# Strassen's algorithm for 8 of 22 pairs of FFN gate/up groups in a two-layer hybrid trunk

## The chip, the cores and the metric

One core of one Trainium2 chip runs the whole computation. The metric is the device time of one execution in microseconds; lower is better. TensorE (PE) multiplies, VectorE (DVE) and ScalarE (ACT) do the element-wise work, GpSimd (POOL) and SyncE (SP) mostly issue DMAs.

## The reference

The input is 256 tokens of 2048 features in float32. Layer 0 has a gated DeltaNet mixer, layer 1 an HGRN2 mixer; each is followed by a SwiGLU FFN, with an RMSNorm ahead of each and residual adds. The change is in the FFN alone:

```python
def swiglu(h, w_gate, w_up, w_down):
    return (jax.nn.silu(h @ w_gate) * (h @ w_up)) @ w_down
...
for layer in range(DEPTH):          # DEPTH = 2
    h = h + mixer(rmsnorm(h, ...))
    h = h + swiglu(rmsnorm(h, ffn_norm[layer]), ffn_w_gate[layer], ffn_w_up[layer], ffn_w_down[layer])
return rmsnorm(h, final_norm)
```

The FFN is 5632 wide, so gate and up are 2048 x 5632 each, and down is 5632 x 2048.

## The kernel before

All weights stream once through the core in *halves*: 128 partitions x 1024 floats, 512 KB. `Trunk.stream` walks over a flat list of them. For each it loads `raw` (a ring of `RAW_BUFS` = 4 buffers, issued from SP), ScalarE copies it to `wh`, rounded to the format that TensorE multiplies, and VectorE makes the rest, `wl = raw - wh`; both have 4 buffers (`SPLIT_BUFS`). Each product of float32 matrices is three matmuls: high by high, high by low, low by high. The activations are split in the same way: `xt_h` and `xt_l` hold the normalized input, transposed.

A *group* of gate/up is 256 gate and 256 up columns (512 together): 8 halves, each with 2 tiles of 128 features x 2 token tiles x 3 = 12 matmuls of 512 columns (`mm_rows`), added up in the two banks of a `main` tile. There are 22 groups in an FFN. At the end of a group (`gate_up`, `end`) ScalarE computes `sg` = silu of the gate, scaled by 1/rms of the row (`rstd`), and VectorE multiplies it by the up part into `h1`. After two groups (a *pair*: 512 hidden features) VectorE transposes `h1` in 16 pieces (`turn`, 32 x 256 each) into `turned`, and the result is split into `hth` and `htl`. They are the operands of the down projection. That comes in two parts (`FF_PARTS`, 12 and 10 groups): after each part, four column groups `cg` of the output are computed, added to the residual `x` (loaded from and stored to `x_home` in DRAM, from Pool's queue), and at the end handed to the next layer.

All operations are first recorded, and `Recorder.plan` then puts them in order: for each engine it takes the operation that is ready by its estimates and is needed earliest, with the streaming matmuls in the order in which they were recorded. The order is fixed before the run; every engine works through its own queue and waits at its head.

Of the kernel before, what the change touches and what calls it, by code (L numbers as in the profile page):

```python
# [8 lines left out]
F32 = mybir.dt.float32  # L9
# [8 lines left out]
P = 128  # L18
# [6 lines left out]
FF_PARTS = (12, 10)  # L25
N_HGRN = 4
LEVELS = (64, 32, 16, 8, 4, 2, 1)
MASKED = LEVELS[2:]
AHEAD = 3
# [465 lines left out]
class Group:  # L495

    def __init__(self, chunks, mm, end, begin=None, apart=False, cols=False):
        self.chunks, self.mm, self.end, self.begin, self.apart = chunks, mm, end, begin, apart  # L500
        self.cols = cols
        self.halves = [
            c[:, at : at + 1024] for c in chunks for at in range(0, c.shape[1], 1024)
        ]


class Trunk:
# [22 lines left out]
    def apart(self):  # L530
        return self.aux(stream=True), self.aux(stream=True)

# [55 lines left out]
    def stream(self, groups):  # L588
        nc = self.nc
        flat = [(g, i) for g in groups for i in range(len(g.halves))]  # L590
        ready = {}

        def place(tag, g):
            w = self.tile(self.wsplit, [P, 1024], tag, F32R, ordered=True)
            v = nc.virtual(w)
            v.pad, v.cols = PAD, g.cols
            return w

        def load(n):
            g, i = flat[n]  # L600
            raw = self.tile(self.wraw, [P, 1024], "raw", ordered=True)
            nc.sync.dma_start(raw, g.halves[i])
            if n == 0:
                nc.ops[-1].lag = 4.2
                nc.edge(self.queue[1], nc.ops[-1])
            h = place("wh", g)
            nc.scalar.activation(h, raw, AF.Copy)
            low = place("wl", g)
# [4 lines left out]
        for n, (g, i) in enumerate(flat):  # L613
            while loaded < min(n + AHEAD, len(flat)):
                load(loaded)
                loaded += 1
            if i == 0:
                if g.begin:
                    g.begin()
                g.ps = self.apart() if g.apart else self.main()  # L620
            g.mm(g.ps, i, *ready.pop(n))
            if i == len(g.halves) - 1:
                g.end(g.ps)
# [143 lines left out]
    def turn(self, out, x):  # L767

        out = out.rearrange("p n (t a s) -> p t n a s", t=2, s=32)
        x = x.rearrange("p t (n b s) -> p t n b s", n=4, s=32)  # L770
        for a in range(4):
            for b in range(4):
                self.nc.vector.transpose(
                    out[32 * b : 32 * b + 32, :, :, a, :], x[32 * a : 32 * a + 32, :, :, b, :]
                )

    def ffn(self, j, after):
        nc, a = self.nc, self.a
        hts, h1s = {}, {}

        def gate_up(gi):
            def end(ps):
                if gi % 2 == 0:
                    h1s[gi // 2] = self.tile(self.pool, [P, 2, 512], "h1", bufs=2)
                h1 = h1s[gi // 2]
                for tt in range(2):
                    col = self.rstd[:, tt : tt + 1]
                    sg = self.tile(self.pool, [P, T], "sg", bufs=2)
                    nc.scalar.activation(sg, ps[:, tt, 0:T], AF.Silu, scale=col)
                    nc.vector.scalar_tensor_tensor(  # L790
                        out=h1[:, tt, gi % 2 * T : (gi % 2 + 1) * T], in0=ps[:, tt, T:512], scalar=col,
                        in1=sg, op0=ALU.mult, op1=ALU.mult,
                    )
                if gi % 2 == 0:
                    return
                turned = self.tile(self.pool, [P, 4, T], "turned", bufs=2)
                self.turn(turned, h1)
                hts[gi // 2] = ht, lt = tuple(
                    self.tile(self.pool, [P, 4, T], f"ht{x}", F32R, bufs=max(FF_PARTS) // 2) for x in "hl"
                )  # L800
                nc.scalar.activation(ht, turned, AF.Copy)
                nc.vector.tensor_tensor(out=lt, in0=turned, in1=ht.bitcast(F32), op=ALU.subtract)

            gu = a[f"ffn_gu{j}"]
            return Group(
                [gu[gi, i] for i in range(4)],
                lambda ps, i, h, l: self.mm_rows(ps, i, h, l, 4, self.operand), end,
            )

        def down(part, cg):  # L810
            first = sum(FF_PARTS[:part]) // 2
            n = FF_PARTS[part] // 2
            w = a[f"ffn_d{j}_{part}"]

            def operand(kt):
                h, l = hts[first + kt // 4]
# [12 lines left out]

            mm = self.mm_apart if apart else self.mm_rows  # L830
            return Group(
                [w[cg, i] for i in range(n)],
                lambda ps, i, h, l: mm(ps, i, h, l, n, operand), end,
                lambda: self.load_x(cg), apart,
            )

        groups = []
        for part, n in enumerate(FF_PARTS):
            lo = sum(FF_PARTS[:part])
            groups += [gate_up(gi) for gi in range(lo, lo + n)]  # L840
            groups += [down(part, cg) for cg in range(4)]
        groups[0].begin = lambda: self.enter(f"ffn{j}")
        return groups
# [439 lines left out]
    def gdn(self, after):  # L1283
        a = self.a
        states = [{} for _ in range(N_HG)]
        groups = []
# [4 lines left out]
        ba = Group([a["gdn_ba"]], self.mm_gates, gates_end)  # L1291
        cols = lambda chunks, end: Group(
# [3 lines left out]
        def part(hg):  # L1296
            st = states[hg]

            def kq_end(ps):
                self.gdn_qk(hg, self.conv_evac(ps), st)  # L1300
                self.gdn_inverse(hg, st)

            def v_end(ps):
                self.gdn_v(hg, ps, st)

            def z_end(ps):
                st["zs"] = zs = self.tile(self.pool, [P, 2, 512], "zs", bufs=2)
# [7 lines left out]
            rows = lambda name, end: Group(  # L1315
                w(name), lambda ps, i, h, l: self.mm_rows(ps, i, h, l, 4, self.operand), end
            )
            return [cols(w("gdn_kq"), kq_end), rows("gdn_v", v_end), rows("gdn_z", z_end)]
# [3 lines left out]
        for kind, n in GDN_ORDER.split():  # L1322
            n = int(n)
            groups += out[n] if kind == "o" else [parts[n]["kvz".index(kind)]]
        groups.insert(0, ba)
        groups[0].begin = self.gdn_setup
        return groups

    def out_proj(self, name, p, states, last, after):
# [9 lines left out]
        def make(cg):  # L1339
# [5 lines left out]
            return Group(  # L1345
# [5 lines left out]
        return [make(cg) for cg in range(4)]  # L1351
# [218 lines left out]
    def hgrn(self, after):  # L1570
        a = self.a
        states = [{} for _ in range(N_HGRN)]
        groups = []

        def part(g):
# [20 lines left out]
            cols = lambda kind, end: Group(  # L1596
                w(kind), lambda ps, i, h, l: self.mm_cols(ps, i, h, l, 2, 4, 4), end, cols=True
            )
            rows = lambda kind, end: Group(
                w(kind), lambda ps, i, h, l: self.mm_rows(ps, i, h, l, 4, self.operand), end  # L1600
            )
            return [cols(1, f_end), cols(0, q_end), rows(2, v_end), rows(3, z_end)]

        for g in range(N_HGRN):
            groups += part(g)
        groups[0].begin = self.hgrn_setup
        groups += self.out_proj("hgrn_out", 0, states, False, after)
        groups += self.out_proj("hgrn_out", 1, states, True, after)
        return groups
# [3 lines left out]
    def finish(self, cg):  # L1613
        nc = self.nc
        if cg == 0:
            self.last = self.tile(self.pool, [P, D], "last")
            nc.gpsimd.dma_start(self.last, self.a["final_norm"].broadcast_to([P, D]))
            self.y = self.tile(self.pool, [P, 2, D], "y")
# [15 lines left out]
    def finish_last(self, ps):  # L1634
# [4 lines left out]
        for tt in range(2):  # L1639
            t = lambda n, tag: self.tile(self.pool, [P, n], f"{tag}{tt}")  # L1640
            x, s3, ss, col = t(512, "xl"), t(1, "s3l"), t(1, "ssl"), t(1, "coll")
# [20 lines left out]
    def run(self):  # L1662
        self.setup()
        self.start(0, True)
        groups = self.gdn(self.next_input(1, False))
        groups += self.ffn(0, self.next_input(2, True))
        groups += self.hgrn(self.next_input(3, False))
        groups += self.ffn(1, self.finish)
        self.stream(groups)
# [92 lines left out]
```

## Time and profile before

| | |
|---|---|
| median of 3 runs | 2764.83 us (2764.65 to 2765.22) |
| profiled execution | 2763.82 us, its span 2761.4 us |
| PE, PEld, DVE, ACT, POOL busy | 99%, 84%, 69%, 52%, 9% |
| HBM read, written | 550.52 MB, 27.31 MB (209 GB/s over the span) |
| mean granted clock of TensorE | 0.999 |

The profile page lists busy times, a timeline in 40 slices, the chain of work that ended last, the costliest groups of instructions and the DMA issues. "wl<-raw,wh" reads: the instruction writes `wl` and reads `raw` and `wh`. Every operation is recorded by one helper, so that all have the same line (L490); they are told apart by the names of their tiles. "Landing" is the time from a DMA's issue to its completion.

### The profile page before, as it was taken

The page shows a single profiled execution, that of the slowest core. Times are in us where ns is not written, and L with a number is a line of the kernel's source. Part 1 is how long each engine was busy: PE and PEld are TensorE (multiplying, and loading weights), DVE is VectorE, ACT ScalarE, POOL GpSimd, SP SyncE. Part 2 cuts the span into 40 slices and gives each one's busy share as a digit, 9 for nine tenths or more (in the row PEclk, how much of TensorE's full clock was granted, in tenths as well). Part 3 has the DMA queues.
Part 4 walks back from the last instruction along what each step waited for, and adds up shares of the span by engine and source line. Part 5 has one row for each costly group of instructions (what it writes and reads, how often), then busy time and mean ns, then how long its engine had stood idle before and what let it go on. Part 6 is the DMA issues. An engine that isn't in the chain of part 4 may idle for free.

```text
span 2761.4 us, 41091 instructions
## 1 busy us (share of the span) xinstructions
PE 2744.9 (99%) x15662; PEld 2328.7 (84%) x15662; DVE 1899.6 (69%) x2857; ACT 1428.3 (52%) x2010; POOL 251.4 (9%) x370
## 2 busy tenths in 40 slices
PE   9999999999999999999999999999999999999998
PEld 9888888888888888888888989988888888888887
DVE  7787888887766667546665687778657675456764
ACT  6646666565554444344444556556454444344443
POOL 1213222232110000000000100000100000000000
PEclk9999999999999999999999999999999999999999
DMA  7686668787786666766667655555776666766664
GB/s 260 201 281 222 190 211 284 210 276 219 225 256 203 195 193 193 225 224 194 193 192 219 221 166 179 172 166 178 236 257 192 193 194 209 224 209 193 193 201 160
DMA packets 162677, 580.52 MB, mean 210 GB/s; under 512 B 20138, under 2 KB 21306, under 8 KB 162352
## 3 DMA queue, kind: packets, MB, share of 16 engines
q1 hardware_dynamic: 138912, 503.15, 57.1%
q0 software_dynamic: 23280, 73.91, 8.5%
q8 instruction: 122, 2.00, 0.3%
q10 hardware_dynamic: 288, 0.85, 0.1%
q14 instruction: 75, 0.61, 0.1%
HBM read 550.52 MB, written 27.31 MB: 209 GB/s over the span
## 4 chain that ended last, share of the span: by engine, by line
PE 98%; ACT 0%; DVE 0%; issue 0%; DMA 0%; SPq 0%; POOLq 0%; POOL 0%; ACTq 0%
PE main L490 92%; PE aux L490 6%; DMA first<-in_x 0%; ACT dec L490 0%; DVE wl L490 0%; ACT wh L490 0%; DVE utmp L490 0%; SPq L490 0%; DVE pre L490 0%; ACT xt_h L490 0%; DVE u L490 0%; ACT y L490 0%; POOLq L1758 0%; ACT junk L490 0%; DVE xl L490 0%
## 5 line engine op out<-in xcount | busy, mean ns | idle before, releaser
L490 DVE TENSOR_TENSOR wl<-raw,wh 128x1024 fp32r<-128x1024 f32 x945 | 1160.6, 1229 | 754.3 <-ACT wh L490 742.6
L490 ACT ACTIVATE wh<-raw 128x1024 fp32r<-128x1024 f32 x945 | 1000.9, 1060 | 1221.8 <-PE main L490 1123.5
L490 PE MATMUL main<-wh,xt_h 128*128 128x512 f32 x2176 | 849.3, 390 | 0.8 <-ACT wh L490 0.8
L490 PE MATMUL main<-wl,xt_h 128*128 128x512 f32 x2176 | 848.5, 390 | 1.3 <-DVE wl L490 1.3
L490 PE MATMUL main<-wh,xt_l 128*128 128x512 f32 x2176 | 849.5, 390 | 0.0
L490 PEld LDWEIGHTS main<-wl,xt_h 128*128 128x128 f32 x2176 | 408.5, 188 | 85.6 <-DVE wl L490 1.6
L490 PEld LDWEIGHTS main<-wh,xt_h 128*128 128x128 f32 x2176 | 408.5, 188 | 85.1 <-ACT wh L490 1.2
L490 PEld LDWEIGHTS main<-wh,xt_l 128*128 128x128 f32 x2176 | 408.6, 188 | 84.5
L490 PE MATMUL main<-xt_h,wh 128*128 128x256 f32 (+1 forms) x1040 | 288.8, 278 | 0.7 <-ACT wh L490 0.7
L490 PE MATMUL main<-xt_h,wl 128*128 128x256 f32 (+1 forms) x1040 | 288.3, 277 | 0.9 <-DVE wl L490 0.9
L490 PE MATMUL main<-xt_l,wh 128*128 128x256 f32 (+1 forms) x1040 | 288.1, 277 | 0.3 <-DVE xt_l L490 0.3
L490 PE MATMUL main<-wh,htl 128*128 128x512 f32 x664 | 258.6, 389 | 0.0
L490 PE MATMUL main<-wl,hth 128*128 128x512 f32 x664 | 258.4, 389 | 0.0
L490 PE MATMUL main<-wh,hth 128*128 128x512 f32 x664 | 258.3, 389 | 0.0
L490 PEld LDWEIGHTS main<-xt_h,wh 128*128 128x128 f32 (+1 forms) x1040 | 194.5, 187 | 1.3 <-ACT wh L490 0.9
L490 PEld LDWEIGHTS main<-xt_h,wl 128*128 128x128 f32 (+1 forms) x1040 | 194.4, 187 | 1.2 <-DVE wl L490 1.1
L490 PEld LDWEIGHTS main<-xt_l,wh 128*128 128x128 f32 (+1 forms) x1040 | 194.4, 187 | 1.0 <-DVE xt_l L490 0.5
L490 DVE STREAM_TRANSPOSE turned<-h 32x256 f32<-32x256 f32 x352 | 153.5, 436 | 7.2
L490 PE MATMUL main<-wh,ot_l 128*128 128x512 f32 x384 | 151.3, 394 | 0.0
L490 PE MATMUL main<-wl,ot_h 128*128 128x512 f32 x384 | 150.5, 392 | 0.0
L490 PE MATMUL main<-wh,ot_h 128*128 128x512 f32 x384 | 150.5, 392 | 0.0
L490 PEld LDWEIGHTS main<-wl,hth 128*128 128x128 f32 x664 | 124.6, 188 | 25.9
(206 smaller groups left out, 2249.9 us busy)
## 6 DMA issues: line engine op xcount, KB each, us to landing
raw<-in_ffn_gu SPq DMA_DIRECT2D x352, 512.0 KB, 4.7
raw<-in_ffn_d SPq DMA_DIRECT2D x176, 512.0 KB, 4.8
raw<-in_hgrn_in SPq DMA_DIRECT2D x128, 512.0 KB, 4.0
raw<-in_gdn_kq SPq DMA_DIRECT2D x64, 512.0 KB, 5.6
raw<-in_gdn_v SPq DMA_DIRECT2D x64, 512.0 KB, 4.7
raw<-in_gdn_z SPq DMA_DIRECT2D x64, 512.0 KB, 4.8
raw<-in_gdn_out SPq DMA_DIRECT2D x64, 512.0 KB, 5.0
x_home<-x POOLq DMA_DIRECT2D x36, 512.0 KB, 6.3
```

The lines of the kernel that those rows point to most:

```text
L490: getattr(getattr(tc.nc, op.eng), op.method)(*args, **kw)
```

## The change

Four of the eleven pairs of each FFN (1, 4, 7 and 8; with two FFNs 8 of 22) are computed by Strassen's algorithm, in the form with shared sums. The 2048 features are cut in two, the 256 tokens in two, and the pair's two groups are the two column blocks: 2 x 2 blocks on each side, seven block products where there were eight. The sums of input blocks (`mixh`, `mixl`) are made once at the start of an FFN, by VectorE and ScalarE, and need the row of 1/rms (`rstd_row`). The sums of weight blocks are made half by half as they stream: of the seven items for one place, three go in as loaded, two are added to by VectorE (`pre`), and two by a second DMA from Pool's queue that adds another half from DRAM to the loaded buffer (`accum_op`). These items have a ring of four buffers of their own (`sraw`); each feeds 6 matmuls. Their products go to four banks `aux` A to D; after the first 16 items three banks are copied aside (`between`), after all 28 the four blocks of the result are put together (`end`).

The items alternate with halves of other groups (`among`, `FF_PLAN`): pair 1 with pairs 2 and 3, pair 4 with the first part of the down projection, and so on. The down projection has three parts now (8, 8 and 6 groups). Eight of the eleven pairs are turned by 4 whole transposes on VectorE, a store to DRAM and four strip loads (`turn_through`); pairs 3, 6 and 10 (`FF_QUICK`) are turned on VectorE in two halves. The list of groups becomes a list of items, each with its own matmuls and ends.

```diff
-FF_PARTS = (12, 10)
+FF_PARTS = (8, 8, 6)
+FF_PLAN = (
+    "0 | 1:2,3",
+    "4:down | 7:5,6",
+    "8:down | 9 | 10",
+)
+FF_QUICK = (3, 6, 10)
...
+def among(few, many, tail):
+    out, done = [], 0
+    for i, item in enumerate(many):
+        out.append(item)
+        upto = min(len(few), -(-len(few) * (i + 1) // (len(many) - tail)))
+        out += few[done:upto]
+        done = upto
+    return out
...
         def load(n):
-            g, i = flat[n]
-            raw = self.tile(self.wraw, [P, 1024], "raw", ordered=True)
-            nc.sync.dma_start(raw, g.halves[i])
+            item = items[n]
+            raw = item.ring() if item.ring else self.tile(self.wraw, [P, 1024], "raw", ordered=True)
+            nc.sync.dma_start(raw, item.src)
...
+            if item.pre:
+                item.pre(raw)
...
+    def turn_through(self, out, x):
+        blocks = self.tile(self.pool, [P, 4, T], "blocks", bufs=1)
+        home = self.tile(self.dram, [P, 4, T], "blocks_home")
...
+        for b in range(4):
+            self.nc.vector.transpose(
+                blocks[:, b, :].rearrange("p (n t s) -> p n t s", n=4, s=32), x[:, :, :, b, :]
+            )
+        self.nc.gpsimd.dma_start(home, blocks)
+        home = home.rearrange("(a f) b r -> b f a r", a=4)
+        for b in range(4):
+            self.nc.gpsimd.dma_start(out[32 * b : 32 * b + 32], home[b])
+
+    def mix_inputs(self):
...
+        for q in range(2):
...
+            for cg in (q, 2 + q):
+                t = self.tile(self.pool, [P, 4, T], "turned", bufs=2, ordered=True)
+                tt(t, self.xt_h[cg].bitcast(F32), self.xt_l[cg].bitcast(F32), ALU.add)
+                tt(t, t, row, ALU.mult)
+                uv += [t[:, :, 0:P], t[:, :, P:T]]
+            a11, a21, a12, a22 = uv
...
+            tt(s1, a21, a22, ALU.subtract)
+            tt(s2, a11, s1, ALU.subtract)
+            tt(s3, a21, a11, ALU.subtract)
+            tt(s4, a12, s2, ALU.subtract)
...
+                nc.scalar.activation(h, sums[n], AF.Copy)
+                tt(low, sums[n], h.bitcast(F32), ALU.subtract)
...
+        def mixed_pair(pair):
...
+            def plus(of, other, kk):
+                def pre(raw):
+                    raws[of] = raw
+                    if other and other[0] == "+":
+                        nc.gpsimd.dma_start(raw, quarter(other[1:], kk), accum_op=ALU.add)
+                    elif other:
+                        nc.vector.tensor_tensor(out=raw, in0=raw, in1=raws[other], op=ALU.add)
+                return pre
...
+                ring = lambda: self.tile(self.pool, [P, 1024], "sraw", bufs=4, ordered=True)
+                return Item(src, mm, plus(of, other, kk), ring=ring)
...
+            def between():
...
+                nc.scalar.activation(sums["p1"], banks["A"], AF.Copy, scale=self.rstd[:, 0:1])
+                nc.vector.tensor_tensor(out=sums["u2"], in0=banks["B"], in1=sums["p1"], op=ALU.subtract)
+                nc.scalar.activation(sums["p5"], banks["C"], AF.Copy)
+                nc.scalar.activation(sums["p4"], banks["D"], AF.Copy, scale=self.rstd[:, 1:2])
...
+            for kk in range(4):
+                items += [
+                    item("11", None, kk, "A", plain(0, 0), True),
+                    item("12", "+11", kk, "C", mixed(1), True),
+                    item("22", "12", kk, "B", mixed(2), True),
+                    item("21", "22", kk, "D", plain(2, 1), True),
+                ]
+            items[0].begin, items[-1].end = begin, between
+            for kk in range(4):
+                items += [
+                    item("21", None, kk, "A", plain(2, 0), False),
+                    item("22", None, kk, "C", mixed(4), False),
+                    item("12", "+22", kk, "B", mixed(3), False),
+                ]
+            items[-1].end = end
...
-        groups = self.gdn(self.next_input(1, False))
-        groups += self.ffn(0, self.next_input(2, True))
+        items = self.gdn(self.next_input(1, True))
+        items += self.ffn(0, self.next_input(2, True))
```

How the queues stand now is shown at three places of the first FFN. The first is VectorE at the entry. Before, after the last `xt_l` (the transposed input's low part) of the gated DeltaNet's end:

```order
L490 TENSOR_REDUCE ss_62<-ssp_61 128x2
L490 TENSOR_SCALAR ss_62<-ss_62 128x2
L490 TENSOR_TENSOR wl_8949<-raw_8839,wh_8933 128x1024
L490 SCALAR_TENSOR_TENSOR xt_l_19_75<-aux_8930,head_63,xt_h_15_71 128x256 x2
L490 SCALAR_TENSOR_TENSOR xt_l_19_75<-aux_8938,head_63,xt_h_15_71 128x256 x2
L490 TENSOR_SCALAR rstdh_60<-rstd_59 128x2
```

Now, a little behind that place (`turned` holds an input block, `h_...` the sums of blocks, `sraw` a Strassen item's half):

```order
L496 TENSOR_TENSOR sraw_8900<-sraw_8900,sraw_8899 128x1024
L496 TENSOR_TENSOR wl_9035<-raw_8958,wh_9023 128x1024
L496 COPY rstd_row_65<-aux_9029 128x256
L496 TENSOR_TENSOR sraw_8901<-sraw_8901,sraw_8900 128x1024
L496 TENSOR_TENSOR turned_8889<-turned_8889,rstd_row_65 128x1024
L496 TENSOR_TENSOR wl_9062<-raw_8983,wh_9049 128x1024
L496 TENSOR_TENSOR turned_8890<-turned_8890,rstd_row_65 128x1024
L496 TENSOR_TENSOR wl_9080<-raw_9004,wh_9066 128x1024
L496 TENSOR_TENSOR h_1320_8891<-turned_8889,turned_8890 128x512
L496 TENSOR_TENSOR h_1321_8892<-turned_8889 128x512
L496 TENSOR_TENSOR wl_9101<-raw_9026,wh_9085 128x1024
```

Between two splits of plain halves there now stand one or two operations of the mixed inputs. The second place is VectorE in the middle of a stretch. Before, at the end of a pair's turn:

```order
L490 STREAM_TRANSPOSE turned_8888<-h_1337_8885 32x2x4x32 x2
L490 TENSOR_TENSOR wl_9368<-raw_9295,wh_9356 128x1024
L490 TENSOR_TENSOR htl_8890<-turned_8888,hth_8889 128x1024
L490 TENSOR_TENSOR wl_9387<-raw_9318,wh_9377 128x1024
L490 TENSOR_TENSOR wl_9408<-raw_9338,wh_9396 128x1024
```

Now, pair 1 beside pair 2, one round and the start of the next:

```order
L496 TENSOR_TENSOR wl_9420<-sraw_9295,wh_9404 128x1024
L496 TENSOR_TENSOR sraw_9364<-sraw_9364,sraw_9337 128x1024
L496 TENSOR_TENSOR wl_9440<-raw_9304,wh_9423 128x1024
L496 TENSOR_TENSOR wl_9448<-sraw_9337,wh_9434 128x1024
L496 TENSOR_TENSOR wl_9467<-raw_9352,wh_9454 128x1024
L496 TENSOR_TENSOR wl_9478<-sraw_9364,wh_9469 128x1024
L496 TENSOR_TENSOR wl_9500<-raw_9382,wh_9490 128x1024
L496 TENSOR_TENSOR wl_9510<-sraw_9394,wh_9502 128x1024
L496 TENSOR_TENSOR wl_9530<-raw_9414,wh_9520 128x1024
L496 TENSOR_TENSOR sraw_9462<-sraw_9462,sraw_9432 128x1024
L496 TENSOR_TENSOR wl_9549<-sraw_9432,wh_9535 128x1024
```

`sraw_9432` takes the buffer of `sraw_9295`, whose last reader is the first row here. Between that row and the addition that reads `sraw_9432` after its accumulating DMA stand eight operations. The third place is Pool's queue beside the first part of the down projection. Before, only the output's stores and loads:

```order
L490 DMA x_11361<-x_home_96 128x2x512
L490 DMA x_home_96<-x_11140 128x2x512
L490 DMA x_11582<-x_home_96 128x2x512
L490 DMA x_home_96<-x_11361 128x2x512
L490 DMA x_11803<-x_home_96 128x2x512
```

Now, with pair 4 in the same stretch:

```order
L496 DMA x_home_96<-x_8863 128x2x512
L496 DMA x_10666<-x_home_96 128x2x512
L496 DMA sraw_10637<-in_ffn_gu 128x1024
L496 DMA sraw_10804<-in_ffn_gu 128x1024
L496 DMA x_home_96<-x_9009 128x2x512
L496 DMA x_10906<-x_home_96 128x2x512
L496 DMA sraw_10900<-in_ffn_gu 128x1024
L496 DMA sraw_10993<-in_ffn_gu 128x1024
```

The accumulating DMAs (`sraw<-in_ffn_gu` on this queue) stand behind the pairs of store and load. Of the gated DeltaNet the order is the same as before up to its last output columns.

More of the change, by code (lines that the diff above doesn't have):

```diff
@@ L531, in apart, with group, first, opening @@
         return self.aux(stream=True), self.aux(stream=True)
+    def group(self, chunks, mm, end, begin=None, apart=False, cols=False):
+        ps, halves = [], halves_of(chunks)
+        def first():
+            if begin:
+                begin()
+            ps.append(self.apart() if apart else self.main())
+        items = [
+            Item(h, lambda wh, wl, i=i: mm(ps[0], i, wh, wl), cols=cols) for i, h in enumerate(halves)
+        ]
+        items[0].begin = first
+        items[-1].end = lambda: end(ps[0])
+        return items
+    def opening(self, items, setup):
+        first = items[0].begin
+        def begin():
+            setup()
+            first()
+        items[0].begin = begin
+        return items
     def setup(self):
@@ L612, in stream @@
         loaded = 0
-        for n, (g, i) in enumerate(flat):
-            while loaded < min(n + AHEAD, len(flat)):
+        for n, item in enumerate(items):
+            while loaded < min(n + AHEAD, len(items)):
                 load(loaded)
                 loaded += 1
[L617 to L623, printed above, removed]
+            if item.begin:
+                item.begin()
+            item.mm(*ready.pop(n))
+            if item.end:
+                item.end()
     def mm_rows(self, ps, i, wh, wl, n_chunks, operand, halves=range(2)):
@@ L794, in end @@
[L794 to L802, printed above, removed]
@@ L813, in down @@
+        def down(part, cg, pairs):
             w = a[f"ffn_d{j}_{part}"]
+            lo = sum(FF_PARTS[:part]) // 2
             def operand(kt):
-                h, l = hts[first + kt // 4]
+                h, l = hts[pairs[kt // 4]]
                 return h[:, kt % 4, :], l[:, kt % 4, :]
@@ L830, in down @@
             mm = self.mm_apart if apart else self.mm_rows
-            return Group(
-                [w[cg, i] for i in range(n)],
+            n = len(pairs)
+            return self.group(
+                [w[cg, p - lo] for p in pairs],
                 lambda ps, i, h, l: mm(ps, i, h, l, n, operand), end,
@@ L1349, in make @@
             )
-        return [make(cg) for cg in range(4)]
+        return [item for cg in range(4) for item in make(cg)]
     def hgrn_setup(self):
```

231 lines of the change are left out of this document (170 added, 61 removed).

## The prediction, on record before the changed kernel ran

> **What bounds the kernel now.** The page first: busy time, then the chain that ended last.
>
> ```profile
> PE 2744.9 (99%) x15662; PEld 2328.7 (84%) x15662; DVE 1899.6 (69%) x2857; ACT 1428.3 (52%) x2010; POOL 251.4 (9%) x370
> PE 98%; ACT 0%; DVE 0%; issue 0%; DMA 0%; SPq 0%; POOLq 0%; POOL 0%; ACTq 0%
> ```
>
> Only TensorE sets the end. Busy matmul time is modelled, so the second view is the chain in order of time: its longest pieces are the two FFNs, the place of the change.
>
> ```profile
> 828.78 636.50 PE main L490 x2808
> 2036.53 687.72 PE main L490 x3034
> ```
>
> That is 687.72/3034 = 0.2267 us per 512-column matmul, without a break (636.50/2808 gives the same). A weight half of a plain group has 12 matmuls: 2.72 us. The third view is the stretches: what the other engines have left.
>
> ```profile
> core 0: us, PE busy (x) PEld busy (x) DVE busy (x) ACT busy (x) POOL busy (x), PEclk, DMA share, GB/s
> 30.00:40.00 10.00, 10.00 (x90) 10.00 (x89) 6.53 (x13) 5.83 (x8) 1.02 (x3) 1.00 0.98 358
> 400.00:500.00 100.00, 100.00 (x687) 84.92 (x686) 84.83 (x184) 63.68 (x118) 33.50 (x51) 1.00 0.82 261
> 2100.00:2200.00 100.00, 100.00 (x443) 82.81 (x442) 65.33 (x81) 44.20 (x49) 0.00 (x0) 1.00 0.61 194
> ```
>
> In the FFN (2100 to 2200) VectorE is 65% busy, ScalarE 44%, and 194 GB/s come in. In the gated DeltaNet (400 to 500) VectorE runs at 85% while TensorE still has no gap, so 85% is bearable. The clock is full. The fourth view, the timeline of one weight half, shows how far ahead the splitting runs:
>
> ```profile
> 2153.09 1.06 ACT L490 ACTIVATE wh<-raw 128x1024 fp32r<-128x1024 f32 x1 [1.66 <-PE main L490]
> 2154.18 1.23 DVE L490 TENSOR_TENSOR wl<-raw,wh 128x1024 fp32r<-128x1024 f32 x1 [1.49 <-ACT wh L490]
> ```
>
> ScalarE waits for TensorE to free one of the four split buffers; 2155.41 - 2153.09 = 2.3 us later (2.5 with the hand-overs) the half is ready, and TensorE comes to it three halves later. Now the lead is 3 x 2.72 - 2.5 = 5.6 us.
>
> **The change, part by part.** *Matmuls removed.* A plain pair of groups has 16 halves x 12 = 192 matmuls; a Strassen pair has 28 items x 6 = 168. Eight pairs save 8 x 24 = 192; 192 x 0.2267 = **-43.5 us**, all on the bounding engine. Two FFN entries now also make the row of 1/rms: two small products each, by the nearest row 4 x 0.272 = **+1.1**.
>
> ```profile
> L490 DVE TENSOR_TENSOR wl<-raw,wh 128x1024 fp32r<-128x1024 f32 x945 | 1160.6, 1229 | 754.3 <-ACT wh L490 742.6
> L490 ACT ACTIVATE wh<-raw 128x1024 fp32r<-128x1024 f32 x945 | 1000.9, 1060 | 1221.8 <-PE main L490 1123.5
> L490 PE MATMUL aux<-head,x 128*128 128x128 f32 x112 | 14.5, 272 | 0.0
> L490 DVE STREAM_TRANSPOSE turned<-h 32x256 f32<-32x256 f32 x352 | 153.5, 436 | 7.2
> L490 DVE TENSOR_TENSOR x<-x,main 128x1024 f32<-128x1024 f32 x39 | 47.6, 1221 | 20.3 <-PE main L490 20.1
> L490 DVE TENSOR_TENSOR e<-b 128x512 f32<-128x512 f32 x48 | 31.4, 682 | 0.0
> ```
>
> *VectorE.* A Strassen item feeds only 6 x 0.2267 = 1.36 us of matmuls but costs one whole split (1.23 us), and two of four in its first half an addition of 1.22 us. Alone it would be bound by VectorE; that is why it stands between plain halves. Four items and four plain halves, as the order alternates them, are one round: 4 x 1.36 + 4 x 2.72 = **16.3 us** of TensorE, against 8 x 1.23 + 2 x 1.22 = 12.3 us of VectorE (75%). Over the kernel: 96 more splits +118 us, 64 additions +78, mixed inputs +41 (below), 5 sums of 0.68 for each of 8 pairs +27, 8 more output additions +10. Turns: now 352 x 0.436 = 153.5; then 16 pairs x 4 whole transposes = 28 and 6 x 32 half ones of at most 0.436 each, at least nothing: I take 0.3, 58 us; about -67. Sum about +207, so 2107 of 2730 (77%), under the 85% that is borne. On the path: nothing, as long as no wait stands in its queue. ScalarE gains 96 x 1.06 = 102 us and stays near 56%.
>
> *Entry of each FFN.* The mixed inputs are 8 operations of 1.22 and 16 of 0.68, 20.7 us. In the order's stretch from the first to the twentieth split, VectorE has 52 us of work (20 splits, these, two additions, the usual rest), TensorE 16 x 2.72 + 4 x 1.36 = 49.0. The 3 us that are missing are covered by the lead of 5.6; waits for 1/rms in the same queue take some of it. 0 to 6 us each, I take 2: **+4**.
>
> *Loads, and the loop through a buffer.* Each Strassen pair loads 28 halves for 16 (96 more on SP's queue), and 8 are added to by a DMA from Pool's queue. They have their own ring of four buffers, and in the first half the second item of each round passes the same buffer every round. The loop: load (L1), accumulating DMA (L2), then an addition and a split on VectorE (2.45) and hand-overs (about 0.45), and the buffer is free: c = L1 + L2 + 2.9. It holds TensorE up if c exceeds 16.3.
>
> ```profile
> raw<-in_ffn_gu SPq DMA_DIRECT2D x352, 512.0 KB, 4.7
> x_home<-x POOLq DMA_DIRECT2D x36, 512.0 KB, 6.3
> x<-x_home POOLq DMA_DIRECT2D x36, 512.0 KB, 5.7
> wide<-n_dram SPq DMA_DIRECT2D x32, 128.0 KB, 7.1
> ```
>
> Those are medians at moderate traffic. A round moves 8 loads + 1 accumulation + about 1.1 halves' worth of turns or x, some 10.1 x 0.524 MB = 5.3 MB in 16.3 us: 324 GB/s. The nearest stretches are two of about 16 us (436 to 452, then 606 to 622 us), each with its packets' line and its issues:
>
> ```profile
> DMA packets 1326, 4.78 MB, mean 299 GB/s; under 512 B 160, under 2 KB 160, under 8 KB 1325
> raw<-in_gdn_out SPq DMA_DIRECT2D x4, 512.0 KB, 6.0
> x_home<-x POOLq DMA_DIRECT2D x1, 512.0 KB, 6.4
> DMA packets 1300, 4.58 MB, mean 286 GB/s; under 512 B 187, under 2 KB 187, under 8 KB 1298
> raw<-in_gdn_z SPq DMA_DIRECT2D x4, 512.0 KB, 6.6
> before<-v_rows POOLq DMA_DIRECT2D x1, 512.0 KB, 9.6
> ```
>
> L1 is 4.7 to 6.6; I take 6.0. No accumulating DMA is in the trace. Below, L2 is a plain Pool load, 5.7; above, two plain transfers one behind the other, 5.7 + 6.3 = 12.0, since it must read the buffer too. I take the loaded plain one, 6.4, plus the time of half a MB at the stretch's own 358 to 299 GB/s less overlap, 1.2: 7.6, nearer to the low rows because most of a landing is latency. Then c = 6.0 + 7.6 + 2.9 = 16.5: 0.2 too long in each of the three returns between four rounds, and the lead (about 3.5 us with short items between) covers 0.6. **0 us** likely. In the second half (period 3 x 1.36 + 3 x 2.72 = 12.2) an accumulation comes into a buffer that a plain item left, so it binds later: two periods, 24.5, against c + 5 for the splits in between.
>
> *Pool's queue.* It stands in order. In the stretches beside the down projection the x load waits for the store before it:
>
> ```profile
> 1153.58 0.73 POOL L490 DMA_DIRECT2D x_home<-x  x1 [24.58 <-DVE x L490]
> 1160.46 0.72 POOL L490 DMA_DIRECT2D x<-x_home  x1 [6.15 <-DMA x_home<-x]
> ```
>
> Behind that wait of 6.15 us accumulations now stand queued, and TensorE behind them; the order leaves a round of work between, so I take nothing here and price it below. The turns through DRAM take a store and four strip loads, by the rows 6.3 + 7.1 + 4 issues, some 16 us, and are read more than 30 us later; where the reader is near (pairs 3, 6, 10) VectorE turns as before. Bank changes between the halves of a pair: 0 to 1 us a pair, I take 0.5: **+4**.
>
> *Sum.* Against the profiled execution's own 2763.82 (span 2761.4 and 2.4 around it): -43.5 + 1.1 + 4 + 0 + 4 = -34.4, so 2729.4. The median of the runs lies 1.0 higher (2764.83): **2730**.
>
> **Rivals.** *A: the accumulating DMA is slow and the loop paces TensorE.* For it: the transfer reads two sources, and no row prices it; the 9.6 us of one plain Pool load shows the tail. At the upper bound, c = 6.0 + 12.0 + 2.9 = 20.9; three returns of 4.6 less the lead of 3.5 = 10.3, and the second half (25.9 - 24.5)/2 x 4 = 2.8: 13.1 us for each of 8 pairs, 105 us, 2730 + 105 = **2835**, slower. It decides from 34.4/8 = 4.3 us a pair, that is c = 18.9, L2 about 10. Against it: all plain Pool medians lie at 5.7 to 6.4. The Trainium skill (Collectives: The Full Stack, section "The bandwidth ceiling: the fold count and why AG ≠ RS ≠ AR") says that an addition inside a DMA costs no cycles of its own, but two source reads through one ring, and so half the rate; no run here shows it. By that rule alone, doubling the whole 6.4 to an estimated 12.8, the sum would be slower still.
>
> *B: the DMA engines are full.* With the accumulation's second read a second-half period moves about (6 + 2 + 0.8) x 0.524 = 4.6 MB in 12.2 us, 378 GB/s; the fullest 10 us above carried 358 at a share of 0.98. At 358 that period takes 12.9: +0.66 x 4 x 8 = 21 us, **2751**, still faster. The Trainium skill (DMA: Bandwidth & Descriptors, "Where 436 GB/s comes from") puts HBM's limit for one core near the same 358, and the fabric's at 435.
>
> *C: Pool's order.* If each of four waits of 6.15 us in the four down stretches falls whole on a landed load, c is 22.6 once: 22.6 - 16.3 - 3.5 = 2.8 us, 16 times, 45 us: **2775**, slower.
>
> That the change doesn't do what it says can be left out: the order has 14212 matmuls for 14400.
>
> **Chances.** Forecast (2720 to 2742) 0.54; B 0.12; A 0.25, by where the plain rows lie; C, wholly or half, 0.07; gains and losses that cancel 0.02. About 0.2%, 5.5 us, is what a measurement can tell from no change. Faster is the forecast and B, 0.66; same is the last and half of C, 0.05; slower 0.29. The range goes from all costs at nothing (2722, rounded to 2720) up into A, to L2 near 11 (c = 19.9: 10.8 - 3.5 + 0.8 = 8.1 a pair, 65 us, 2795) and a little over: 2810. The rest of A, about 0.13, is left out.
>
> **What would show it.** Right: 192 matmuls fewer at 0.2267 each in the FFN stretches, TensorE without idle there, accumulating DMAs landing in 7 to 9 us, VectorE near 80%. Rival A: landings over 10 us, and TensorE idle behind VectorE and ScalarE, which wait for a DMA into sraw, mostly in the first half of a pair. B: a DMA share of 0.95 or more, with plain loads landing late too. C: such waits only beside the down projection. The forecast is wrong if TensorE's idle time in the two FFNs is over 40 us.

## The result, and the profile after

The changed kernel takes **2808.31 us** (median of 4 runs, 2806.01 to 2814.63); the kernel before took 2764.74 us (4 runs, 2763.53 to 2765.22) on the same chip. The ratio is 1.0162, 95% interval 1.0144 to 1.018: slower by 43.6 us, where 35 us less were forecast. The profiled execution took 2806.91 us, its span 2805.2.

Busy times on the page of the kernel after:

```profile
PE 2735.5 (98%) x15478; PEld 2298.7 (82%) x15478; DVE 2059.4 (73%) x3029; ACT 1537.7 (55%) x2152; POOL 366.3 (13%) x530
```

There are 184 matmuls fewer, which is the 192 and the added small products, but PE's busy time fell only by 9.4 us, and its idle time grew from 2761.4 - 2744.9 = 16.5 to 2805.2 - 2735.5 = 69.7 us. Where: the table by stage, the two FFNs up to the last gate/up half, first of the kernel before, then of the kernel after.

```profile
824.56:1546.28 721.72, 721.72 (x3201) 598.09 (x3200) 445.80 (x522) 318.22 (x351) 12.39 (x17) 1.00 0.65 205
2032.31:2751.06 718.75, 718.75 (x3176) 595.24 (x3175) 442.69 (x515) 312.57 (x339) 10.59 (x15) 1.00 0.63 200
```

```profile
824.05:1568.27 744.22, 716.93 (x3109) 583.50 (x3108) 525.66 (x608) 372.87 (x422) 69.31 (x97) 0.99 0.85 272
2054.31:2794.84 740.53, 714.81 (x3084) 580.68 (x3083) 522.98 (x601) 367.09 (x410) 67.44 (x95) 0.99 0.83 268
```

The first number is the stretch, the second PE's busy time in it. Before there was no gap; now TensorE idles 27.3 and 25.7 us, and the DMA share has gone from 0.65 to 0.85. The stages outside the FFNs kept their lengths. Landings, from the list of DMA issues of the kernel after (the last number is the median in us), and two groups of the table of waits (sum, count, longest):

```profile
raw<-in_ffn_gu SPq DMA_DIRECT2D x224, 512.0 KB, 5.9
sraw<-in_ffn_gu SPq DMA_DIRECT2D x224, 512.0 KB, 6.8
sraw<-in_ffn_gu POOLq DMA_DIRECT2D x64, 512.0 KB, 9.4
```

```profile
ACT wh L496 <- DMA sraw<-in_ffn_gu: 217.8, 47, 9.4
DVE sraw L496 <- DMA sraw<-in_ffn_gu: 61.3, 20, 8.0
```

The accumulating transfer lands after 9.4 us, and ScalarE, whose `wh` begins every split, waits for such blocks. One loop through a buffer can be followed in the timeline, pair 4 near its end; the load's buffer is known from the order's names. First SP's and Pool's issues, then the time that these two transfers took to land, from the list of DMA issues cut to them:

```profile
1093.47 0.33 SPq L496 DMA_DIRECT2D raw<-in_ffn_d  x1
1099.39 0.33 SPq L496 DMA_DIRECT2D sraw<-in_ffn_gu  x1
1100.53 0.33 SPq L496 DMA_DIRECT2D raw<-in_ffn_d  x1
1101.66 0.33 SPq L496 DMA_DIRECT2D sraw<-in_ffn_gu  x1
1102.80 0.33 SPq L496 DMA_DIRECT2D raw<-in_ffn_d  x1
1103.93 0.33 SPq L496 DMA_DIRECT2D sraw<-in_ffn_gu  x1
1106.20 0.33 SPq L496 DMA_DIRECT2D raw<-in_ffn_d  x1
...
1116.97 0.87 POOL L496 DMA_DIRECT2D sraw<-in_ffn_gu  x1 [10.88 <-ACT wh L496]
1128.62 0.33 SPq L496 DMA_DIRECT2D sraw<-in_ffn_gu  x1
```

```profile
sraw<-in_ffn_gu SPq DMA_DIRECT2D x1, 512.0 KB, 12.5
sraw<-in_ffn_gu POOLq DMA_DIRECT2D x1, 512.0 KB, 9.2
```

Then ScalarE and VectorE in the same 20 us:

```profile
1115.87 1.06 ACT L496 ACTIVATE wh<-raw 128x1024 fp32r<-128x1024 f32 x1 [1.66 <-PE main L496]
1126.28 1.06 ACT L496 ACTIVATE wh<-sraw 128x1024 fp32r<-128x1024 f32 x1 [9.36 <-DMA sraw<-in_ffn_gu]
1116.96 1.23 DVE L496 TENSOR_TENSOR wl<-raw,wh 128x1024 fp32r<-128x1024 f32 x1 [1.36 <-ACT wh L496]
1127.37 1.23 DVE L496 TENSOR_TENSOR wl<-sraw,wh 128x1024 fp32r<-128x1024 f32 x1 [9.19 <-ACT wh L496]
```

The load of 1103.93 lands at 1103.93 + 12.5 = 1116.4. The accumulation is issued at 1116.97, half a microsecond later (the view puts down as its releaser the `wh` that ended at 1116.93). It lands at 1126.2, `wh` starts at 1126.28, `wl` ends at 1128.60, and at 1128.62 the buffer is loaded again: 24.7 us where the prediction had c = 16.5. The item is the last of its pair, so it stands in the second half. For 9 us both splitting engines stand still with plain halves ready behind. What that costs TensorE, by the table of stretches there:

```profile
1117.00:1127.00 10.00, 6.99 (x31) 5.45 (x29) 1.19 (x1) 0.72 (x1) 2.44 (x3) 1.00 1.05 349
1127.00:1135.00 8.00, 6.85 (x22) 5.30 (x23) 7.63 (x8) 5.42 (x8) 0.00 (x0) 0.79 0.80 231
1129.00:1132.00 3.00, 3.00 (x8) 2.35 (x8) 3.00 (x4) 1.84 (x3) 0.00 (x0) 0.50 0.73 234
```

TensorE is idle for 3.0 us in the first stretch and 1.2 in the second. In the 8 us from 1127 on the granted clock is 0.79, and from 1129 to 1132 it is 0.50: a gap is paid once as idle time and again as slower matmuls.

### The profile page after: what moved, and what is told of

It is laid out like the page before. It is cut to its first block, busy times and chain, and to the rows that moved or that the text cites. A ratio compares the mean times of both kernels' runs of the same rounds, so it can differ in the third digit from the quotient of the medians.

```text
span 2805.2 us, 41692 instructions
## 1 busy us (share of the span) xinstructions
PE 2735.5 (98%) x15478; PEld 2298.7 (82%) x15478; DVE 2059.4 (73%) x3029; ACT 1537.7 (55%) x2152; POOL 366.3 (13%) x530
## 5 line engine op out<-in xcount | busy, mean ns | idle before, releaser
L496 ACT ACTIVATE wh<-raw 128x1024 fp32r<-128x1024 f32 x817 | 861.4, 1058 | 804.2 <-PE main L496 699.4
L496 DVE TENSOR_TENSOR wl<-raw,wh 128x1024 fp32r<-128x1024 f32 x817 | 999.9, 1226 | 400.9 <-ACT wh L496 392.7
L496 PE MATMUL main<-wl,xt_h 128*128 128x512 f32 x1664 | 653.2, 393 | 11.5 <-DVE wl L496 11.5
L496 PE MATMUL main<-wh,xt_h 128*128 128x512 f32 x1664 | 653.1, 393 | 4.9 <-ACT sg L496 4.1
L496 PE MATMUL main<-wh,xt_l 128*128 128x512 f32 x1664 | 652.7, 392 | 0.0
L496 ACT ACTIVATE wh<-sraw 128x1024 fp32r<-128x1024 f32 x224 | 236.7, 1058 | 303.0 <-DMA sraw<-in_ffn_gu 217.8
L496 DVE TENSOR_TENSOR wl<-sraw,wh 128x1024 fp32r<-128x1024 f32 x224 | 272.7, 1220 | 174.8 <-ACT wh L496 169.6
L496 PEld LDWEIGHTS main<-wh,xt_l 128*128 128x128 f32 x1664 | 314.2, 189 | 64.7
L496 PEld LDWEIGHTS main<-wh,hth 128*128 128x128 f32 x680 | 128.4, 189 | 32.1 <-ACT hth L496 5.4
L496 PEld LDWEIGHTS main<-wh,htl 128*128 128x128 f32 x680 | 128.1, 188 | 31.2 <-DVE htl L496 4.9
```

The lines of the kernel that those rows point to most:

```text
L496: getattr(getattr(tc.nc, op.eng), op.method)(*args, **kw)
```

## The experiments

Four theories. **1**: the loop through one of four buffers is too long for the round. **2**: the accumulating transfer burdens the DMA engines. **3**: accumulations wait in Pool's queue. **4**, formed after the first runs: the planner wrote the order for a landing of 6.5 us on Pool's queue (`LANDING`), so what needs a late block stands too early in ScalarE's and VectorE's queues and blocks what is behind it. The kernel before took 2763.1 to 2764.2 us beside each of these runs.

**What the second transfer costs.** e1: it overwrites and does not add. e2: it is left out. Both leave the weight sum out, 8 of 28 items of a pair.

```diff
-nc.gpsimd.dma_start(raw, quarter(other[1:], kk), accum_op=ALU.add)
+nc.gpsimd.dma_start(raw, quarter(other[1:], kk))          # e1; e2: no line
```

> The second transfer of the 8 items a pair overwrites instead of adding (the weight sums are left out there): same queue, same bytes from DRAM, same waits, only the addition's read of the buffer is gone. Theory 1 (the loop through a Strassen buffer: load 6.8 + accumulation 9.4 + 2.9 = 19.1 us against 16.3 of matmuls), with the second read as the slow part: landing falls from 9.4 to about 7.5, time to 2760-2780. Theory 2 (the DMA engines are full, every transfer is late): 8 half reads of about 76 a stretch less, landing stays at 8.5 or more, time 2790-2805. Theory 3 (Pool's order: accumulations stand behind turns and x loads): no change, 2800-2810.

> The second transfer is left out altogether (so the weight sums of those items are), all else stays. Theory 1: the loop is 6.8 + 2.9 = about 10 us, no wait is left, 2722 plus some 8 at the entries: 2725-2740. Theory 2: of the stretches' bytes some 12 to 20 percent go, plain loads still land late (6 to 7 us), 2750-2780. Theory 3: also 2725-2740, since nothing that matters stands behind the turns any more.

e1: 2748.49 us (ratio 0.9944, 0.9929 to 0.9959). e2: 2736.93 us (0.9902, 0.9887 to 0.9916). So everything else in the change comes near its forecast, and of the 71 us that the second transfers cost, 60 go with the addition in them. The overwriting transfer lands in 7.9 us, the accumulating one in 9.4.

**The additions on another engine.** e3 adds on VectorE, e6 on GpSimd, from a second block in SBUF that is loaded anyway.

```diff
-nc.gpsimd.dma_start(raw, quarter(other[1:], kk), accum_op=ALU.add)
+nc.vector.tensor_tensor(out=raw, in0=raw, in1=raws[other[1:]], op=ALU.add)   # e3
+nc.gpsimd.tensor_tensor(out=raw, in0=raw, in1=raws[other[1:]], op=ALU.add)   # e6
```

> All weight sums on VectorE: the accumulating DMA becomes an addition of the other buffer, which is still loaded (result complete). 64 more additions of 1.22 us, 78 us of VectorE, a round then has 8 x 1.23 + 3 x 1.22 = 13.5 of 16.3 us. Theories 1 and 3: loop gone, 2725-2745, under the time before. Theory 2: as without the second transfer, 2750-2780. A fourth, that VectorE is the next bound: VectorE over 88 percent busy in the stretches, 2750-2790, with TensorE waiting for wl and no DMA ahead of it.

> The 64 accumulating DMAs become additions on GpSimd of the buffer that is loaded already (result complete), 128x1024 each; no row shows such an addition, the plan's estimate is 2.4 us. Theories 1 and 3: the loop is 6 + 2.5 + 2.9 = 11.4 us, and VectorE gets nothing more: 2732-2750. If GpSimd's additions hold VectorE up while they run, VectorE's splits get longer than 1.23 us and the time is 2755-2790.

e3: 2762.70 us (median of 10 runs, 2757.12 to 2770.15; 1.000, 0.9988 to 1.0012): no gain is left. A stretch of e3 in the first FFN:

```profile
884.00:994.00 110.00, 108.11 (x478) 89.19 (x477) 89.24 (x93) 62.60 (x68) 5.53 (x10) 1.00 0.83 272
```

VectorE is 81% busy, its additions wait 102.7 us for blocks over the kernel, and TensorE has gaps (1.9 of 110 us). e6: **2750.05 us** (0.9949, 0.9934 to 0.9965), faster than before. An addition takes 2.83 us on GpSimd, and VectorE pays a little beside it (the blocks' splits of the kernel after first, 1220 ns, then the groups of e6):

```profile
L496 DVE TENSOR_TENSOR wl<-sraw,wh 128x1024 fp32r<-128x1024 f32 x224 | 272.7, 1220 | 174.8 <-ACT wh L496 169.6
```

```profile
L496 DVE TENSOR_TENSOR wl<-raw,wh 128x1024 fp32r<-128x1024 f32 x817 | 1048.7, 1286 | 425.1 <-ACT wh L496 415.8 <-PE aux L496 3.0 <-PE main L496 2.0
L496 DVE TENSOR_TENSOR wl<-sraw,wh 128x1024 fp32r<-128x1024 f32 x224 | 306.9, 1372 | 33.5 <-ACT wh L496 28.0
L496 POOL TENSOR_TENSOR sraw<-sraw,sraw 128x1024 f32<-128x1024 f32 x64 | 181.1, 2830 | 514.3 <-DMA sraw<-in_ffn_gu 453.1 <-DVE x L496 18.4 <-DVE h L496 16.4
```

**Half of the accumulations.** e7 does only the first half's additions on VectorE, e8 only the second half's; the others stay in DMAs.

```diff
+if other == "+22":     # e7; e8: "+11"
     nc.gpsimd.dma_start(raw, quarter(other[1:], kk), accum_op=ALU.add)
+else:
+    nc.vector.tensor_tensor(out=raw, in0=raw, in1=raws[other[1:]], op=ALU.add)
```

> Only the sums of the first half of a pair (12+11) go to VectorE; those of the second half stay accumulating DMAs. Theory 1 (a buffer that takes an accumulation each round, in the first half only): nearly all waits go, 2755-2770, with 32 additions more on VectorE. If every accumulating DMA costs alike: half of the way from 2808 to 2763, 2780-2790.

> The other way round: only the sums of the second half (12+22) go to VectorE; those of the first half stay accumulating DMAs. Theory 1: the loop of the first halves stays, 2790-2805. If every accumulating DMA costs alike: 2780-2790, as with the first halves.

e7: 2804.57 us (1.0145, 1.0129 to 1.0161); e8: 2819.09 us (1.0196, 1.0181 to 1.0212). With half as many accumulations the time is as long as with all, so the loss is not so much per transfer, and it is not in one half of the pair alone. But these runs do not price a transfer by itself: e3 shows that additions on VectorE cost time too, and the table under "What is left" shows how much in each half.

**A fifth buffer.** e4 makes its room by a block tile from the ring `turned`; e5 by keeping `u2` in a spare tile and one buffer less for `sg`.

```diff
-ring = lambda: self.tile(self.pool, [P, 1024], "sraw", bufs=4, ordered=True)
+ring = lambda: self.tile(self.pool, [P, 1024], "sraw", bufs=5, ordered=True)
```

> Five buffers in the ring of the Strassen items instead of four; to make room, the block tile of a turn comes from the ring of the turned tiles. All transfers stay. Theory 1: a buffer now comes round after five items, 20.4 us, over the 19.1 of the loop: most of the 86 us of waits go, 2735-2755. Theory 2: the engines are as full as before, 2790-2810. Theory 3: the waits behind turns stay, 2770-2790.

> Five Strassen buffers again, with the room taken elsewhere (one sum is kept in the dump tile of the square sums, the silu tile has one buffer), so that the turns are as in the changed kernel. All transfers stay. Theory 1 (the loop through one buffer, 19.1 us against 16.3): five items are 20.4 us, most of the first halves' waits go, 2745-2765. Theory 2 (the DMA engines are full): 2795-2810.

e4: 2810.55 us (1.0168, 1.0153 to 1.0183), but its turns came late (TensorE waited up to 11.6 us for `hth`), so its total tells little about the ring. e5: 2798.91 us (1.0129, 1.0113 to 1.0146), only 9 us better. ScalarE's waits for blocks went from 217.8 to 22.6 us, VectorE's additions now wait instead (91.8 us).

**The order, and both.** e9 tells the planner 9.0 us for an accumulating transfer; e10 does that with five buffers; e11 is e6 with five buffers.

```diff
 nc.gpsimd.dma_start(raw, quarter(other[1:], kk), accum_op=ALU.add)
+nc.ops[-1].lag = 9.0
```

> The whole edit: the planner that writes out the order is told 9.0 us instead of 6.5 us for the landing of an accumulating transfer; every addition stays with the transfers and the buffers stay four, so the order of VectorE, ScalarE and TensorE moves but no work does. Theory 4 (the order was written for 6.5 us, so splits and additions that need a late block stand at the head of VectorE's and ScalarE's queues and block the splits behind them): 2760 to 2780 us, and ScalarE's waits of wh for the DMA of sraw fall from 217.8 us to under 100. Theory 1 (a buffer's loop of 6.8 + 9.4 + 2.9 = 19.1 us against a round of 16.3 us): the loop is as long as before, 2795 to 2810 us, the waits move to SP's queue. Theory 2 (the accumulating transfers as such slow the loads): 2795 to 2810 us with raw still landing at 7 to 8 us in the stretches.

> The planner's 9.0 us for the accumulating transfer and a fifth buffer for block quarters together. If theory 4 and theory 1 each hold a part of the loss: 2740 to 2765 us, near the kernel whose second transfer only overwrites (2748.5 us). If theory 4 alone: as with the 9.0 us alone, within 5 us. If the accumulating transfers themselves hold the DMA engines (theory 2): 2785 us or more.

> The additions on GpSimd (2750.1 us with four buffers) and a fifth buffer. If late buffers are what is left over the kernel without second transfers (2736.9 us): 2738 to 2746 us. If what is left is the second load's traffic and the longer splits of VectorE beside GpSimd: 2746 to 2755 us, as with four.

e9: 2816.56 us (1.0184, 1.0167 to 1.0201), slower still. e10: **2749.48 us** (0.995, 0.9935 to 0.9964), with all additions in accumulating DMAs. e11: **2745.54 us** (0.9931, 0.9916 to 0.9945), the fastest complete version. Waits for blocks in e9, then in e10, and e10's landing:

```profile
ACT wh L496 <- DMA sraw<-in_ffn_gu: 151.3, 41, 7.6
DVE sraw L496 <- DMA sraw<-in_ffn_gu: 35.7, 17, 4.2
```

```profile
ACT wh L496 <- DMA sraw<-in_ffn_gu: 30.1, 19, 4.4
DVE sraw L496 <- DMA sraw<-in_ffn_gu: 25.9, 15, 4.4
...
sraw<-in_ffn_gu POOLq DMA_DIRECT2D x64, 512.0 KB, 8.6
```

The fitting order alone costs 8 us more, the fifth buffer alone brings 9, both together 59: on the total, theories 1 and 4 hold only jointly (by halves they part, see the table below). How long a loop is depends on the loads too, which bunch behind a stall. Loads matched to their accumulations: from a load's issue to its accumulation's in the kernel after, median 5.8 us in first halves and 9.2 (up to 14.6) in second halves. In the timeline above SP stands from 1093.8 to 1099.4, until a buffer is free, and then issues six loads in 7 us; the one at 1103.93 is the fifth of them, took 12.5 us, and made the next split late. A run that only spreads the loads was not made.

**What is left.** e12 is e10 with transfers that overwrite (the 8 of 28 sums left out); e13 and e14 are e7 and e8 with the 9.0 us.

> As the kernel with 9.0 us for the accumulating transfer and five buffers (2749.5 us), but the second transfer overwrites the buffer and does not add (8 of 28 weight sums of a Strassen pair are left out). If only the latency of an accumulating transfer costs anything, and five buffers with the order that fits have hidden it (theories 1 and 4): within 5 us of 2749.5 us. If the addition in the transfer also takes time from the DMA engines (theory 2): faster by 8 us or more, under 2742 us.

> First-half additions on VectorE, second-half ones by accumulating transfers that the planner takes as 9.0 us, four buffers. With the order for 6.5 us this took 2804.6 us. By the prediction's loop arithmetic the second half binds only from a loop of 19.5 us, and here it is 5.9 + 9.2 + 2.9 = 18.0, so if the order was what cost (theory 4) it falls to 2750 to 2770 us. If four buffers are too few in the second half as well: 2795 us or more.

> The other way round: second-half additions on VectorE, first-half ones by accumulating transfers that the planner takes as 9.0 us, four buffers. With the order for 6.5 us this took 2819.1 us. If the loop through a buffer in the first half (18.2 us or more, against a round of 16.3 us) is what paces TensorE (theory 1), the fitting order does not help: 2790 us or more. If the order alone decided (theory 4): 2750 to 2775 us.

e12: 2733.49 us (0.9892, 0.9877 to 0.9906). With five buffers and 9.0 us an overwriting second transfer costs nothing that shows (e2, without any, took 2736.93); one that adds takes 2749.48 - 2733.49 = 16 us more. That is what theory 2 foretold, but the traces do not put it on full DMA engines: e10 still waits 30.1 + 25.9 us for blocks (above), e12 4.2 us, and the table below finds the difference in the first halves alone. The same 120 us of the first FFN in e10, then in e12:

```profile
884.00:1004.00 120.00, 119.64 (x528) 98.76 (x528) 94.05 (x107) 67.71 (x74) 14.60 (x22) 1.00 0.96 307
```

```profile
884.00:1004.00 120.00, 120.00 (x531) 99.41 (x530) 95.12 (x110) 68.47 (x74) 12.62 (x23) 1.00 0.91 304
```

The issues and landings of the second transfers, in e10 and then in e12 (of an issue group the second number is the mean in ns that it holds Pool's queue):

```profile
L496 POOL DMA_DIRECT2D sraw<-in_ffn_gu x64 | 56.8, 888 | 643.5 <-DMA sraw<-in_ffn_gu 341.6 <-DVE wl L496 128.3 <-DVE sraw L496 74.9
```

```profile
PE 2706.5 (99%) x15478; PEld 2293.5 (84%) x15478; DVE 2075.3 (76%) x3029; ACT 1550.2 (57%) x2152; POOL 343.1 (13%) x530
L496 POOL DMA_DIRECT2D sraw<-in_ffn_gu x64 | 35.2, 550 | 645.6 <-DMA sraw<-in_ffn_gu 315.0 <-DVE wl L496 202.8 <-DVE sraw L496 51.5
sraw<-in_ffn_gu POOLq DMA_DIRECT2D x64, 512.0 KB, 7.6
```

At about the same GB/s the accumulating version holds the DMA engines at a share of 0.96 for 0.91. e13: 2785.52 us (1.0076, 1.0047 to 1.0105); e14: 2780.99 us (1.0066, 1.0051 to 1.0081). Both missed: the fitting order brings 19 and 38 us, less than theory 4 alone would give and more than theory 1 alone.

How the loss splits can be read from the starts of the Strassen matmuls (those that write `aux`) in each profiled execution. A first half runs from the first matmul of item 1 to that of item 17, a second half from there to the last matmul of item 28. The table has the time beyond that of e12, in us, summed over the eight pairs; the rest of the span is in the last column.

| | buffers, planner's landing | second transfers | first halves | second halves | rest |
|---|---|---|---|---|---|
| after | 4, 6.5 | all add | 22.4 | 42.5 | 6.7 |
| e9 | 4, 9.0 | all add | 31.0 | 53.7 | -0.8 |
| e5 | 5, 6.5 | all add | 38.5 | 0.0 | 23.0 |
| e10 | 5, 9.0 | all add | 12.0 | 0.1 | 1.6 |
| e1 | 4, 6.5 | all overwrite | 14.9 | 0.8 | -2.2 |
| e7 | 4, 6.5 | second half; first on VectorE | 16.1 | 47.2 | 5.2 |
| e13 | 4, 9.0 | second half; first on VectorE | 17.1 | 33.2 | 4.3 |
| e8 | 4, 6.5 | first half; second on VectorE | 46.4 | 35.1 | 2.5 |
| e14 | 4, 9.0 | first half; second on VectorE | 34.8 | 11.8 | -3.4 |

In the second halves the ring decides: with a fifth buffer nothing is lost, whatever the order (e5, e10, and e4 as well), with four the fitting order does not help while all the transfers add (e9), and with four and the shorter landing of an overwriting transfer (7.9 us, e1) almost nothing is lost. In the first halves it takes both: the buffer alone (e5) and the order alone (e9, e14) leave over 30 us, both leave 12. The second half of pair 1 in the kernel after, in e5 and in e10:

```profile
935.36:987.29 51.93, 47.99 (x205) 38.58 (x204) 29.20 (x32) 25.77 (x29) 6.34 (x10) 0.98 0.96 298
942.18:988.20 46.02, 46.02 (x205) 38.10 (x204) 29.44 (x30) 26.99 (x29) 6.33 (x9) 1.00 1.00 323
934.34:980.35 46.01, 46.01 (x204) 38.11 (x203) 31.20 (x34) 26.82 (x29) 6.32 (x9) 1.00 1.02 326
```

With five buffers the DMA engines are at a share of 1.00 and more there, and TensorE has no gap. Whether a sixth buffer would take what is left of the first halves in e10 stays open.

## Why the prediction was wrong

- *Matmuls removed* (-43.5): right. e12, with the same matmuls, is 30.0 us faster than before, against -34.4 forecast with entries and bank changes (+4 each). By the matmul starts of e12 the two entries cost 3.0 us, the bank changes show no gap over 0.5 us, and the down projections that begin beside pairs 4 and 8 wait 2.2 us each for `hth` and `htl`: four times, 8.9 us that the sum did not have.
- *VectorE* (2107 us, 77%): right in kind, 2059.4 us. The half transposes came out at 303 ns (192 of them, 58.1 us), as taken. That 85% is borne did not carry over: at 81%, with waits for blocks in VectorE's queue, e3 lost the gain; which of the two it was, no run parts. In the kernel after VectorE is 71% busy in the FFNs, and waits for `wh`.
- *Loads, and the loop through a buffer* (0 us): **this is the step that failed.** It took c = 6.0 + 7.6 + 2.9 = 16.5 us in both halves, and the loads as even. L2 measured 9.4. L1, from a load to its accumulation's issue, measured 5.8 in first halves but 9.2 in second ones, where loads bunch. So in the second half c = 9.2 + 9.4 + 2.9 = 21.5, over the 19.5 from which the prediction's own formula binds: (26.5 - 24.5)/2 x 4 = 4.0 us a pair, 32 for eight, and 42.5 were measured (with the slower clock behind the gaps). The formula holds there: in e1, measured in the same way, c = 7.3 + 7.9 + 2.9 = 18.1 stays under 19.5, and 0.8 us were lost. In the first half c = 5.8 + 9.4 + 2.9 = 18.1 gives 3 x 1.8 - 3.5 = 1.9 us a pair, 15 for eight, and 22.4 were measured. But there the formula does not tell it all, since five buffers alone did not help (e5): the order, written for a landing of 6.5 us, holds up splits behind late blocks (VectorE's additions wait 91.8 us for them in e5 and 25.9 in e10), and for that the sum had no term.
- *The clock* had no term either. In span, the kernel after is 2805.2 - 2733.6 = 71.6 us longer than e12: 69.7 - 27.1 = 42.6 more of idle TensorE and 2735.5 - 2706.5 = 29.0 more of busy time for the same 15478 matmuls. Of these 29.0, about 14 are the clock, by the mean granted clock of each (0.993 of 2805.2 us and 0.998 of 2733.6). The rest is stalls that the page counts as busy, since it draws a matmul of 512 columns with 0.39 us where the next starts 0.23 us behind it.
- *Rival A* named this mechanism, and the stated range reaches up to 2810 only because of it; that 2808.3 lies inside is no success of the forecast. Rival A's signs came in part. TensorE's idle time did stand behind waits for a DMA into `sraw`, but more of the loss was in the second halves than in the first, and the landings stayed under 10 us: with late loads 9.4 is enough. The point of decision, L2 of about 10, was set too high, with loads taken as even and the clock and the order left out. The Trainium skill (Collectives: The Full Stack, "The bandwidth ceiling: the fold count and why AG ≠ RS ≠ AR") gives two source reads, and so half the rate, for the addition in a reduce-scatter, from which the prediction drew its 12.8. The trace does not show a doubled landing: 8.6 us in e10 beside 7.6 overwriting in e12, and a share of 0.96 beside 0.91.
- *Rival B* (DMA engines full): at most the 16 us between e12 and e10, and not in the second halves, for which it was worked out: e10 lost 0.1 us there, and in pair 1 it has a share of 1.02 without a gap. *Rival C* (Pool's order): seen at one place, where an accumulation stood behind a turn that waited 8.9 us for its store; no run priced it by itself.
- The stated sign of failure, over 40 us of idle TensorE in the FFNs, came: 27.3 + 25.7 = 53.0 us.

## What to carry to other kernels

A ring of buffers is long enough when its loop, with the landing times of the crowded stage and not of the quiet one, is shorter than the time between two uses, with room for loads that bunch after a late one. If an order is fixed ahead of time, a new kind of transfer needs its own landing time in the planner, together with the buffers that this time calls for: either alone may gain little, as here 9 and -8 us, and 59 together. Count a gap on TensorE at more than its length, here about 1.25 times (71.6 us, of which some 14 are the slower clock, for the other 57).

## What the runs showed of the hardware

- An accumulating DMA of 512 KB into SBUF landed in 8.6 us where an overwriting one on the same queue took 7.6; its issue held Pool's queue 0.89 us instead of 0.55 (e10 and e12).
- Behind the stall at 1124 us the granted clock was 0.79 over 8 us, a loss of 8 x 0.21 = 1.7 us, which is 3.4 us at half the clock. The Trainium skill (TensorE: Matmul & The Clock Gate, "What's actually happening") lets the clock fall to half after an idle window of 3.413 us; half of one such window is 1.7 us, and the trace agrees with that length. It does not need a wholly idle window, as another stall of the kernel after shows: with 1.17 of 3.41 us busy, and no gap over 1.5 us, the clock fell to 0.50 for the next 3.41 us.

```profile
982.01:985.42 3.41, 1.17 (x5) 0.40 (x4) 1.29 (x2) 2.38 (x4) 0.00 (x0) 1.00 1.04 278
985.42:988.83 3.41, 3.41 (x8) 2.73 (x9) 3.41 (x6) 2.24 (x3) 0.00 (x0) 0.50 0.66 192
```

- An addition of 128x1024 numbers took 2.83 us on GpSimd (e6), and beside these VectorE's splits of blocks took 1372 instead of 1220 ns on average. The Trainium skill (SBUF — State Buffer, "Who interferes with whom") says that a VectorE instruction with two inputs in SBUF contends with a GpSimd one that reads SBUF; the trace agrees, at 12%.
